# A two-layer encoder trunk on TensorE: combinations issued in steps, tiles 5 to 19 with seven products

## The chip, the cores and the metric

The kernel runs on one core of one Trainium2 chip. The metric is the device time of one execution in microseconds (us). Of the engines, TensorE (PE in the profile) multiplies, VectorE (DVE) and ScalarE (ACT) do elementwise work, GpSimd (POOL) a few squares at the start, and SyncE (SP) issues the loads and stores. PEld is the loading of weights into TensorE, which overlaps its products.

## The reference

Two layers, each a feed-forward stage, a mixer and a second feed-forward stage, on 512 positions of 1024 channels in float32. What matters here is the feed-forward stage, which comes four times:

```python
def swiglu(h, w_gate, w_up, w_down):
    return (jax.nn.silu(h @ w_gate) * (h @ w_up)) @ w_down

for l in range(DEPTH):                      # DEPTH = 2
    f1 = swiglu(rmsnorm(x, ffn1_pre_g[l]), ffn1_w_gate[l], ffn1_w_up[l], ffn1_w_down[l])
    x = x + 0.5 * rmsnorm(f1, ffn1_post_g[l])
    ...                                     # x = x + rmsnorm(mixer_block(rmsnorm(x, ...)), mix_post_g[l])
    f2 = swiglu(rmsnorm(x, ffn2_pre_g[l]), ffn2_w_gate[l], ffn2_w_up[l], ffn2_w_down[l])
    x = x + 0.5 * rmsnorm(f2, ffn2_post_g[l])
```

The hidden width is 2816, so 22 tiles of 128 hidden channels.

## The kernel before, in words

Every float32 operand is cut into a high and a low part (`fp32r`); a product is three matmuls, high by high, high by low and low by high. Weights arrive from memory as raw units of 128 x 1024 (512 KB, one SP DMA each, two pair buffers `raw`). `Weights.prep` cuts them into the tiles `w`, up to AHEAD = 4 steps before they are taken: ACT writes the high part (L163), DVE the low part (L164).

A feed-forward stage (`ffn`) walks over three groups of 7, 7 and 8 hidden tiles. After each group the down projection runs over 8 output tiles (`pd`, and `po` in the last group). There are three ways to make a hidden tile:

- The first three tiles of a stage run in two halves of 256 positions (`hidden` with `halfgemm`, L330 and L331): first all three for the first half, then all three for the second, so that the stage can begin when the first half of its input is there.
- A full tile runs `gemm` twice, for gate and up: 8 blocks x 3 matmuls x 2 = 48 matmuls of 512 columns.
- A tile in the list SEVEN runs `seven`: gate and up and the two position halves form a 2 by 2 block problem that takes seven block products in place of eight, 7 x 4 x 3 = 84 matmuls of 256 columns. It needs sums of weight blocks, made on DVE when the raw unit is cut (L191 to L193, L197, then L201 on ACT and L202 on DVE), and four combinations of input blocks (`comb`), which `combine` makes once a stage. PSUM parts are read between products by ACT (`keep`, L465), and the tile ends on DVE (L478 to L483) and with the cut of `h` (L339 ACT, L340 DVE).

In the kernel before, `combine` is called by the first tile of SEVEN, tile 3, right after the half tiles. It scales the inputs (L427 to L429), forms sums in two buffers of `fa` (L430, L431, L433) and cuts the four results (L436 on ACT, L437 on DVE, 128 x 1024 each).

The order on each engine is set by a list scheduler, which goes through the instructions in the order in which the Python code issues them and lets a ready one pass one that it believes is not ready. Each engine then works its list in order.

At the start, SP loads the first half of x in four pieces, between them the first three weight units, then the second half of x. TensorE runs 12 matmuls of ones (L261) until the first operands are cut. At the end, each output tile of the last stage is added to `fa` in two DVE adds (L561, L562), squared on ACT (L565) and summed into `acc` (L572); a matmul with ones (L353) sums over the partitions, and a chain on ACT and DVE scales the result and stores it (L357 to L382).

Of the kernel before, what the change touches and what calls it, by code (L numbers as in the profile page):

```python
# [9 lines left out]
F32 = mybir.dt.float32  # L10
# [5 lines left out]
L = 2  # L16
# [9 lines left out]
SEVEN = (3, 4, 6, 7, 8, 10, 11, 13, 14, 15, 17, 18, 19)  # L26
AHEAD = 4
LEAD = 3
WARM = 12
# [96 lines left out]
class Weights:  # L126
# [19 lines left out]
    def load(self, pieces=1):  # L146
        i, n = self.loaded, self.units[self.loaded][1]
        if i % 2 == 0:
# [65 lines left out]
def trunk(ctx: ExitStack, tc: tile.TileContext, xt: bass.AP, cst: bass.AP, rows: bass.AP, ws: bass.AP, wp: bass.AP, out: bass.AP):  # L214
# [111 lines left out]
    def halfgemm(ps, w, a, n, ts, ks=None):  # L326
# [23 lines left out]
    def rstd(acc, r, load, steps, eps=None):  # L350
# [64 lines left out]
    def ffn(l, f, xn, rn, acc, fa, end, first):  # L415
# [5 lines left out]
        def combine():  # L421

            q = [v[:, :, :].rearrange("p a (b t) -> p (a b) t", b=2).rearrange("p (u k) t -> p u k t", u=2) for v in fa]
            b12, b22, d, t3 = q[0][:, 0], q[0][:, 1], q[1][:, 0], q[1][:, 1]
            gx = {1: C_F1PRE, 2: C_F2PRE}[f]
            for k in range(4):
# [7 lines left out]
            for v, sign in ((b22, -1.0), (d, 1.0), (t3, 1.0), (b12, -1.0)):  # L434
# [51 lines left out]
        def hidden(m, h, wg, wu, ts, n, first=None):  # L486
# [19 lines left out]
        for gi, g in enumerate(GROUPS):  # L506
# [345 lines left out]
```

## Time and profile before

| | us |
|---|---|
| median of 3 runs (lowest to highest) | 2496.9 (2495.53 to 2497.68) |
| the profiled execution, its own time | 2496.67 |
| its span, first to last instruction | 2494.9 |
| TensorE busy in the span | 2460.0 (99%) |
| VectorE busy | 1658.5 (66%) |
| ScalarE busy | 1223.8 (49%) |

The time of the profiled execution is 1.8 us over its span. TensorE's share of 99% says that it is the engine to follow; matmuls overlap in the pipeline and their ends are modelled, so the share does not show short waits or a lower clock. These are read from single stretches.

### The profile page before, as it was taken

What the parts mean: (1) busy time and instruction counts of PE and PEld (TensorE: products, weight loads), DVE (VectorE), ACT (ScalarE), POOL (GpSimd) and SP (SyncE); (2) the same over time, 40 slices, a digit from 0 to 9 for tenths busy, and PEclk for the clock granted to TensorE, in tenths of its full rate; (3) what the DMA queues carried; (4) which work ended last, traced back from release to release, by engine and by line L of the source; (5) the groups of instructions that cost most, each with busy time, mean ns of one, the idle gap of its engine ahead of it and who ended that gap; (6) DMA issues with size and microseconds to landing.
All of it is one profiled execution on the core that took longest, in us unless ns stands there. A gap on an engine that the chain in (4) does not pass through costs nothing.

```text
span 2494.9 us, 33879 instructions
## 1 busy us (share of the span) xinstructions
PE 2460.0 (99%) x13720; PEld 2155.5 (86%) x13720; DVE 1658.5 (66%) x2480; ACT 1223.8 (49%) x2038; POOL 4.8 (0%) x8
## 2 busy tenths in 40 slices
PE   8999999999999999999999999999999999999998
PEld 7898989888888888989888989898888888889896
DVE  8676774843874586657785667749357846856575
ACT  6443554334773564435564434533357626644343
POOL 0000000000000000000000000000000000000000
PEclk9999999999999999999999999999999999999999
DMA  3323323222223313233212323322213232123231
GB/s 138 110 100 112 119 101 102 81 88 102 90 80 118 118 35 110 100 111 117 88 66 98 110 89 117 130 82 88 101 69 119 89 114 102 49 97 111 87 118 48
DMA packets 69565, 243.52 MB, mean 98 GB/s; under 512 B 7712, under 2 KB 7840, under 8 KB 69408
## 3 DMA queue, kind: packets, MB, share of 16 engines
q1 hardware_dynamic: 69264, 241.20, 27.7%
q8 instruction: 107, 1.75, 0.3%
q14 instruction: 50, 0.41, 0.1%
q10 hardware_dynamic: 144, 0.15, 0.0%
HBM read 239.23 MB, written 2.10 MB: 97 GB/s over the span
## 4 chain that ended last, share of the span: by engine, by line
PE 91%; DVE 5%; ACT 1%; DMA 1%; issue 1%; SPq 0%; DVEq 0%; ACTq 0%
PE po L330 7%; PE pu L309 6%; PE pu L310 6%; PE pu L311 6%; PE pg L310 4%; PE pg L311 4%; PE pg L309 4%; PE pd L309 4%; PE pd L310 4%; PE pd L311 4%; PE po L331 4%; PE pmg L311 3%; PE pmg L309 3%; PE pmg L310 3%; PE py L311 2%; PE py L309 2%
## 5 line engine op out<-in xcount | busy, mean ns | idle before, releaser
L164 DVE TENSOR_TENSOR w<-raw,w 128x1024 fp32r<-128x1024 f32 (+2 forms) x405 | 479.6, 1198 | 155.4 <-ACT w L163 153.3
L163 ACT ACTIVATE w<-raw 128x1024 fp32r<-128x1024 f32 (+2 forms) x405 | 409.0, 1032 | 167.3 <-DMA raw<-wp 58.1
L309 PE MATMUL pg<-xn,w 128*128 128x256 f32 (+1 forms) x608 | 193.1, 318 | 0.0
L310 PE MATMUL pg<-xn,w 128*128 128x256 f32 (+1 forms) x608 | 192.6, 317 | 0.0
L311 PE MATMUL pg<-xn,w 128*128 128x256 f32 (+1 forms) x608 | 192.4, 316 | 0.0
L330 PE MATMUL po<-h,w 128*128 128x512 f32 x512 | 180.2, 396 | 0.0
L309 PE MATMUL pd<-h,w 128*128 128x512 f32 x448 | 174.4, 389 | 0.0
L310 PE MATMUL pd<-h,w 128*128 128x512 f32 x448 | 174.4, 389 | 0.0
L311 PE MATMUL pd<-h,w 128*128 128x512 f32 x448 | 174.3, 389 | 0.0
L309 PE MATMUL pmg<-xn,w 128*128 128x512 f32 x384 | 149.4, 389 | 0.0
L310 PE MATMUL pmg<-xn,w 128*128 128x512 f32 x384 | 149.4, 389 | 0.0
L311 PE MATMUL pmg<-xn,w 128*128 128x512 f32 x384 | 149.4, 389 | 0.0
L331 PE MATMUL po<-h,w 128*128 128x256 f32 x512 | 144.7, 283 | 0.0
L201 ACT ACTIVATE w<-raw 128x512 fp32r<-128x512 f32 x208 | 120.8, 622 | 48.4 <-DVE raw L193 23.6
L202 DVE TENSOR_TENSOR w<-raw,w 128x1024 fp32r<-128x1024 f32 x104 | 125.0, 1222 | 23.6 <-ACT w L201 23.3
L309 PE MATMUL pu<-comb,w 128*128 128x256 f32 x416 | 123.0, 296 | 14.3 <-ACT comb L436 13.5
L311 PE MATMUL pu<-xn,w 128*128 128x256 f32 (+1 forms) x400 | 133.6, 334 | 0.0
L310 PE MATMUL pu<-xn,w 128*128 128x256 f32 (+1 forms) x400 | 133.5, 334 | 0.0
L309 PE MATMUL pu<-xn,w 128*128 128x256 f32 (+1 forms) x400 | 133.4, 334 | 0.0
L310 PE MATMUL pu<-comb,w 128*128 128x256 f32 x416 | 120.7, 290 | 2.7 <-DVE comb L437 2.7
L311 PEld LDWEIGHTS pg<-xn,w 128*128 128x128 f32 x608 | 115.9, 191 | 8.1 <-DVE w L164 0.5
L309 PEld LDWEIGHTS pg<-xn,w 128*128 128x128 f32 x608 | 115.9, 191 | 7.1
(260 smaller groups left out, 6396.0 us busy)
## 6 DMA issues: line engine op xcount, KB each, us to landing
raw<-wp SPq DMA_DIRECT2D x391, 512.0 KB, 4.3
raw<-wp SPq DMA_DIRECT2D x64, 448.0 KB, 4.1
x<-xt SPq DMA_DIRECT2D x8, 256.0 KB, 6.6
out<-x SPq DMA_DIRECT2D x8, 256.0 KB, 2.1
rw<-rows SPq DMA_DIRECT2D x6, 256.0 KB, 3.6
raw<-wp SPq DMA_DIRECT2D x2, 256.0 KB, 4.2
rw<-ws SPq DMA_DIRECT2D x2, 256.0 KB, 4.0
c<-cst ACTq DMA_DIRECT2D x1, 148.0 KB, 4.0
```

The lines of the kernel that those rows point to most:

```text
L163: self.nc.scalar.activation(out=hi, in_=raw, func=AF.Copy)
L164: self.nc.vector.tensor_tensor(out=lo, in0=raw, in1=hi.bitcast(F32), op=ALU.subtract)
L201: self.nc.scalar.activation(out=v[:, 0, b], in_=r[:, n], func=AF.Copy)
L202: self.nc.vector.tensor_tensor(out=v[:, 1], in0=r[:, 0::3] if key[0] == "s1" else r[:, 1:3], in1=v[:, 0].bitcast(F32), op=ALU.subtract)
L309: nc.tensor.matmul(out=ps, lhsT=w_hi, rhs=a_hi, start=first, stop=False, skip_group_check=on)
L310: nc.tensor.matmul(out=ps, lhsT=w_hi, rhs=a_lo, start=False, stop=False, skip_group_check=on)
L311: behind(nc.tensor.matmul(out=ps, lhsT=w_lo, rhs=a_hi, start=False, stop=last, skip_group_check=on))
L330: nc.tensor.matmul(out=ps.rearrange("p (a t) -> p a t", a=2), lhsT=w[:, 0, o:o + 128], rhs=a(k, slice(0, 2), ts), start=k == 0, stop=False)
L331: behind(nc.tensor.matmul(out=ps[:, :HS], lhsT=w[:, 1, o:o + 128], rhs=a(k, 0, ts), start=False, stop=k == n - 1))
```

## The change

Four edits.

1. `combine` becomes a generator, begun before the second half of the half tiles. Its parts are issued after the half tiles 1 and 2 and after each full tile of the first group, in place of all at once in tile 3. Two of the four cuts come after tile 3, two after tile 4. The buffers in `fa` are laid out otherwise; the operations and their sizes are the same.
2. SEVEN is 5 to 19 (15 tiles a stage) in place of 13 tiles from 3 to 19. Tiles 3 and 4 become full tiles, tiles 5, 9, 12 and 16 become seven-product tiles.
3. At the start the first weight unit is loaded in two halves, before and after the second piece of x; units 1 to 3 come after the whole first half of x. 16 matmuls of ones run first, and three more after every second block of the first gate product. The four scalings of constants (L274) wait until the second half of the input is cut.
4. In the last output tile of the second half of the last stage, `gemm` puts all 24 matmuls into one PSUM half, so that one DVE add is enough, and its square goes straight into a second matmul with ones in place of the add to `acc`.

```diff
-SEVEN = (3, 4, 6, 7, 8, 10, 11, 13, 14, 15, 17, 18, 19)
+SEVEN = (5, 6, 7, 8, 9, 10, 11, 12, 13, 14, 15, 16, 17, 18, 19)
-WARM = 12
+WARM = 16
...
             nc.sync.dma_start(out=x_[k // 4][:, h, k % 4:k % 4 + 2], in_=xt[:, h, k:k + 2])
-            if h == 0 and k in (0, 4, 6):
-                wt.load(2 if k == 0 else 1)
+            if h == 0 and k < 4:
+                wt.load(1, 2, k // 2)
+        for i in range(3 if h == 0 else 0):
+            wt.load()
...
+    def busy(n):
+
+        for _ in range(n):
+            nc.tensor.matmul(out=warm[:, :P], lhsT=ones, rhs=ones, start=True, stop=True)
...
+            if k % 2 and k < n - 1:
+                busy(fill)
...
-        mm = nc.tensor.matmul(out=ps, lhsT=ones, rhs=acc, start=True, stop=True)
+        mm = nc.tensor.matmul(out=ps, lhsT=ones, rhs=acc, start=True, stop=more is None)
+        if more is not None:
+            mm = nc.tensor.matmul(out=ps, lhsT=ones, rhs=more, start=False, stop=True)
...
+            yield
             nc.vector.tensor_tensor(out=t3, in0=b22, in1=b12, op=ALU.subtract)
             nc.vector.tensor_tensor(out=b22, in0=b22, in1=d, op=ALU.add)
+            yield
+            parts(b22, -1.0)
+            parts(d, 1.0)
+            yield
+            parts(t3, 1.0)
...
+            parts(b12, -1.0)
+            yield
 
         def seven(m, h):
 
-            if not comb:
-                combine()
...
-                    halfgemm(a, w, xn, KD, ts)
+                    halfgemm(a, w, xn, KD, ts, fill=3 if first and a is pg else 0)
...
+            steps = combine()
             for m in range(skew):
                 hidden(m, h, *ws_[m], HALVES[1], HS)
+                if m > 0:
+                    next(steps)
             for m in range(skew, g):
                 if m0 + m in SEVEN:
                     seven(m, h)
                     continue
                 hidden(m, h, wt.take(("gate", f, l, m0 + m)), wt.take(("up", f, l, m0 + m)), FULL, S)
+                if gi == 0:
+                    next(steps)
...
-                    halfgemm(ps, ws_[d], h, g, ts)
+                    if s and d == 7 and tail:
+                        gemm(ps[:, :HS], ws_[d], h, g, ts)
+                    else:
+                        halfgemm(ps, ws_[d], h, g, ts)
...
-                    nc.vector.tensor_tensor(out=dst, in0=dst, in1=ps[:, HS:], op=ALU.add)
+                    if not (s and d == 7 and tail):
+                        nc.vector.tensor_tensor(out=dst, in0=dst, in1=ps[:, HS:], op=ALU.add)
...
+                elif s and d == 7 and tail:
+                    more = sq
```

How the order moves is seen best in the second feed-forward stage of the first layer. On DVE before, from the end of the half tiles into tile 3 (`comb` are the cut combinations, `a22l` and `raw` the weight unit of tile 4, `fa` the combinations under way, `sg` and `h` the end of the half tiles):

```order
764 L340 TENSOR_TENSOR h<-sg,h 128x256
765 L429 SCALAR_TENSOR_TENSOR fa<-x,c,fa 128x256
766 L430 TENSOR_TENSOR fa<-fa 128x1024
767 L164 TENSOR_TENSOR a22l<-raw,a22h 128x512
768 L431 TENSOR_TENSOR fa<-fa 128x1024
769 L191 TENSOR_TENSOR raw<-raw 128x512
770 L433 SCALAR_TENSOR_TENSOR fa<-x,c,fa 128x256 x4
771 L437 SCALAR_TENSOR_TENSOR comb<-fa,comb 128x1024 x4
772 L192 TENSOR_TENSOR raw<-raw 128x512
```

On DVE now, at the end of tile 3 (its last sum is 790, its `h` 793; `w` and `raw` belong to tile 5):

```order
790 L525 TENSOR_TENSOR sg<-sg,pu 128x512
791 L204 TENSOR_TENSOR w<-raw,w 128x1024
792 L444 SCALAR_TENSOR_TENSOR comb<-fa,comb 128x1024
793 L351 TENSOR_TENSOR h<-sg,h 128x512
794 L444 SCALAR_TENSOR_TENSOR comb<-fa,comb 128x1024
795 L199 TENSOR_TENSOR raw<-raw 128x512
```

Two of the four cuts stand here now. On DVE now, at the end of tile 4 (its last sum is 803, its `h` 806; `w` and `raw` belong to tile 6):

```order
803 L525 TENSOR_TENSOR sg<-sg,pu 128x512
804 L195 TENSOR_TENSOR raw<-raw 128x512
805 L199 TENSOR_TENSOR raw<-raw 128x512
806 L351 TENSOR_TENSOR h<-sg,h 128x512
807 L444 SCALAR_TENSOR_TENSOR comb<-fa,comb 128x1024 x2
808 L204 TENSOR_TENSOR w<-raw,w 128x1024 x2
```

The four cuts stood in one piece between the half tiles and the first tile of SEVEN; the last two now stand behind the last sum of tile 4, ahead of tile 6's weights. On ACT at the same place now (`pt` and `vp` are the reads of PSUM between the products of tile 5):

```order
592 L522 ACTIVATE sg<-sg 128x512
593 L350 ACTIVATE h<-sg 128x512
594 L443 ACTIVATE comb<-fa 128x1024 x2
595 L203 ACTIVATE w<-raw 128x512 x4
596 L165 ACTIVATE w<-raw 128x896
597 L487 ACTIVATE pt<-pu 128x256
598 L487 ACTIVATE vp<-pg 128x256
599 L487 ACTIVATE pt<-pu 128x256
```

Two cuts of combinations and five cuts of weights stand ahead of tile 5's first read of PSUM, behind the end of tile 4. On SP the start before, and then now:

```order
1 L253 DMA x<-xt 128x512
2 L154 DMA raw<-wp 128x512 x2
3 L253 DMA x<-xt 128x512 x2
4 L154 DMA raw<-wp 128x1024
5 L253 DMA x<-xt 128x512
6 L154 DMA raw<-wp 128x1024
7 L253 DMA x<-xt 128x512 x4
```

```order
1 L255 DMA x<-xt 128x512
2 L154 DMA raw<-wp 128x512
3 L255 DMA x<-xt 128x512
4 L154 DMA raw<-wp 128x512
5 L255 DMA x<-xt 128x512 x2
6 L154 DMA raw<-wp 128x1024 x3
7 L255 DMA x<-xt 128x512 x4
```

The four pieces of the first half of x are now issued ahead of all whole weight units, and a third whole unit ahead of the second half of x.

## Rows read from the trace of the kernel before

**Rows 1.** The page's busy times of the whole span.
```profile
PE 2460.0 (99%) x13720; PEld 2155.5 (86%) x13720; DVE 1658.5 (66%) x2480; ACT 1223.8 (49%) x2038; POOL 4.8 (0%) x8
```

**Rows 2.** Windows, second feed-forward stage: tile 8; tile 9; tiles 17 to 19.
```profile
core 0: us, PE busy (x) PEld busy (x) DVE busy (x) ACT busy (x) POOL busy (x), PEclk, DMA share, GB/s
...
1016.36:1026.43 10.07, 10.07 (x86) 10.07 (x85) 9.55 (x15) 7.61 (x13) 0.00 (x0) 1.00 0.29 104
1026.43:1037.34 10.91, 10.91 (x50) 9.02 (x49) 8.03 (x12) 2.42 (x4) 0.00 (x0) 1.00 0.28 98
...
1148.23:1179.10 30.87, 30.87 (x254) 30.44 (x253) 22.89 (x31) 18.25 (x33) 0.00 (x0) 1.00 0.35 119
```

**Rows 3.** Windows: tiles 3, 4 and 5 in each of the four stages.
```profile
45.50:84.10 38.60, 35.00 (x218) 31.92 (x217) 32.41 (x52) 22.15 (x43) 0.00 (x0) 0.91 0.16 51
918.20:958.10 39.90, 34.61 (x218) 31.71 (x217) 34.69 (x56) 24.11 (x47) 0.00 (x0) 0.91 0.16 56
1280.90:1320.20 39.30, 34.41 (x218) 31.41 (x217) 34.70 (x56) 24.12 (x47) 0.00 (x0) 0.91 0.17 57
2153.90:2193.70 39.80, 34.53 (x219) 31.64 (x218) 34.81 (x56) 24.22 (x47) 0.00 (x0) 0.91 0.16 56
```

**Rows 4.** Waits of the whole span: total us, times, longest.
```profile
PE pu L309 <- ACT comb L436: 13.5, 4, 3.9
```

**Rows 5.** Windows: the low clock in tile 3, second stage.
```profile
928.54:935.36 6.82, 5.84 (x25) 5.55 (x26) 6.75 (x8) 3.25 (x6) 0.00 (x0) 0.50 0.00 0
```

**Rows 6.** Timeline (start, us, what), tile 3 of the second stage, DVE and ACT.
```profile
923.77 1.23 DVE L430 TENSOR_TENSOR fa<-fa 128x1024 f32<-128x1024 f32 x1
...
928.83 4.62 DVE L437 SCALAR_TENSOR_TENSOR comb<-fa,comb 128x1024 fp32r<-128x1024 f32 x4
...
926.82 3.90 ACT L436 ACTIVATE comb<-fa 128x1024 fp32r<-128x1024 f32 x4 [2.31 <-DVE fa L431]
```

**Rows 7.** Groups by line: count, busy us, mean ns of one.
```profile
L202 DVE TENSOR_TENSOR w<-raw,w 128x1024 fp32r<-128x1024 f32 x104 | 125.0, 1222 | 23.6 <-ACT w L201 23.3
...
L480 DVE TENSOR_TENSOR sg<-sg,rn 128x512 f32<-128x512 f32 x52 | 35.8, 688 | 1.0
...
L483 DVE SCALAR_TENSOR_TENSOR sg<-sg,vp 128x256 f32<-128x256 f32 x52 | 21.8, 418 | 0.0
```

**Rows 8.** Timeline of DVE, tiles 17 to 19 of the second stage.
```profile
1158.78 0.69 DVE L480 TENSOR_TENSOR sg<-sg,rn 128x512 f32<-128x512 f32 x1
1159.38 0.69 DVE L164 TENSOR_TENSOR a22l<-raw,a22h 128x512 fp32r<-128x512 f32 x1
...
1166.18 1.22 DVE L164 TENSOR_TENSOR w<-raw,w 128x1024 fp32r<-128x1024 f32 x1
1167.32 0.42 DVE L478 TENSOR_TENSOR vp<-vp 128x256 f32<-128x256 f32 x1
...
1169.89 0.42 DVE L483 SCALAR_TENSOR_TENSOR sg<-sg,pu 128x256 f32<-128x256 f32 x1 [0.70 <-ACT sg L481]
```

**Rows 9.** Timeline of the start: PE, ACT.
```profile
1.05 5.49 PE L261 MATMUL warm<-ones 128*128 128x128 f32 x24 [1.05 <-DVE ones L258]
6.46 0.70 PE L330 MATMUL pg<-xn,w 128*128 128x512 f32 x1
...
14.03 0.40 PE L330 MATMUL pu<-xn,w 128*128 128x512 f32 x1
...
10.09 0.91 ACT L388 ACTIVATE xn<-x,c 128x256 fp32r<-128x256 f32 x2 [0.94 <-DMA x<-xt]
```

**Rows 10.** Windows: the start's stretch at the low clock.
```profile
10.36:13.77 3.41, 3.24 (x9) 2.44 (x10) 3.41 (x6) 3.41 (x7) 0.81 (x1) 0.50 1.06 404
```

**Rows 11.** Chain of waits at the end: start, us, what.
```profile
2482.00 0.43 DVE fa L561
...
2483.36 0.44 DVE acc L572
2483.84 0.71 PE st L353 x2
```

More of the change, by code (lines that the diff above doesn't have):

```diff
@@ L151, in load @@
         of = self.wp[self.off:self.off + P * n].rearrange("(p n) -> p n", p=P)
-        for j in range(pieces):
-            part = slice(n * j // pieces, n * (j + 1) // pieces)
-            self.nc.sync.dma_start(out=raw[:, part], in_=of[:, part])
+        part = slice(n * a // pieces, n * (a + count) // pieces)
+        self.nc.sync.dma_start(out=raw[:, part], in_=of[:, part])
+        if a + count < pieces:
+            return
         self.raw[i] = self.pair
@@ L259, in trunk @@
     warm = st_p.tile([P, S], F32, tag="st", name="warm")
-    for i in range(WARM):
-        nc.tensor.matmul(out=warm[:, :P], lhsT=ones, rhs=ones, start=i == 0, stop=i == WARM - 1)
+    def busy(n):
+        for _ in range(n):
+            nc.tensor.matmul(out=warm[:, :P], lhsT=ones, rhs=ones, start=True, stop=True)
+    busy(WARM)
     def col(l, j):
@@ L267, in after, with halved @@
         tc.add_manual_dep(a.ins, b.ins.name, mybir.DependencyInfo(mybir.DependencyClass.NoSync, mybir.DependencyReason.DATA), reason="table set")
-    def halved():
+    def halved(last):
         for l in range(L):
@@ L273, in halved @@
                 v = c[:, l * NC + j:l * NC + j + 8]
-                nc.vector.tensor_scalar(out=v, in0=v, scalar1=0.5, scalar2=None, op0=ALU.mult)
+                after(nc.vector.tensor_scalar(out=v, in0=v, scalar1=0.5, scalar2=None, op0=ALU.mult), last)
     def derived(last):
@@ L324, in gemm, with halfgemm @@
             mm3(ps, w[:, 0, o:o + 128], w[:, 1, o:o + 128], a(k, 0, ts), a(k, 1, ts), k == 0, k == n - 1)
-    def halfgemm(ps, w, a, n, ts, ks=None):
+    def halfgemm(ps, w, a, n, ts, ks=None, fill=0):
         for k in ks or range(n):
@@ L348, in roots, with rstd @@
         return load
-    def rstd(acc, r, load, steps, eps=None):
+    def rstd(acc, r, load, steps, eps=None, more=None):
         ps = st_p.tile([P, S], F32, tag="st", name="st")[:, :HS]
-        mm = nc.tensor.matmul(out=ps, lhsT=ones, rhs=acc, start=True, stop=True)
+        mm = nc.tensor.matmul(out=ps, lhsT=ones, rhs=acc, start=True, stop=more is None)
+        if more is not None:
+            mm = nc.tensor.matmul(out=ps, lhsT=ones, rhs=more, start=False, stop=True)
         later.append([steps, mm])
@@ L372, in bc, with post @@
         return v[:, None, :].to_broadcast([P, 2, HS])
-    def post(fa, acc, ts, load, store):
+    def post(fa, acc, ts, load, store, more=None):
         r = t2("r1")[:, :HS]
-        rstd(acc[:, ts], r, load, 0 if store else 4 if ts is HALVES[0] else 9)
+        rstd(acc[:, ts], r, load, 0 if store else 4 if ts is HALVES[0] else 9, more=more)
         for n, (i, js) in enumerate(PAIRS):
@@ L388, in cut @@
             nc.scalar.activation(out=xn(k, 0, ts), in_=yk, func=AF.Copy, scale=gk)
-            nc.vector.scalar_tensor_tensor(out=xn(k, 1, ts), in0=yk, scalar=gk, in1=xn(k, 0, ts).bitcast(F32), op0=ALU.mult, op1=ALU.subtract)
+            low = nc.vector.scalar_tensor_tensor(out=xn(k, 1, ts), in0=yk, scalar=gk, in1=xn(k, 0, ts).bitcast(F32), op0=ALU.mult, op1=ALU.subtract)
+        return low
     def scale(ts, scratch, r, steps, load=False, first=False, eps=None):
@@ L421, in combine, with parts @@
         def combine():
-            q = [v[:, :, :].rearrange("p a (b t) -> p (a b) t", b=2).rearrange("p (u k) t -> p u k t", u=2) for v in fa]
+            q = [v.rearrange("p (u b) (k t) -> p u (b k) t", u=2, k=2) for v in fa]
             b12, b22, d, t3 = q[0][:, 0], q[0][:, 1], q[1][:, 0], q[1][:, 1]
             gx = {1: C_F1PRE, 2: C_F2PRE}[f]
+            def parts(v, sign):
+                t = slot_p.tile([P, 2, 4, HS], F32R, tag="slot", name="comb")
+                nc.scalar.activation(out=t[:, 0], in_=v, func=AF.Copy, scale=sign)
+                nc.vector.scalar_tensor_tensor(out=t[:, 1], in0=v, scalar=sign, in1=t[:, 0].bitcast(F32), op0=ALU.mult, op1=ALU.subtract)
+                comb.append(t)
             for k in range(4):
@@ L537, in out_halves @@
     def out_halves(l, gp, g, h, key, fa, acc, add, end):
-        ws_ = []
+        ws_, more, tail = [], None, key[:3] == ("down", 2, L - 1)
         for s, ts in enumerate(HALVES):
@@ L570, in out_halves @@
                     nc.vector.scalar_tensor_tensor(out=acc[:, ts], in0=acc[:, ts], scalar=E8, in1=sq, op0=ALU.add, op1=ALU.add)
+                elif s and d == 7 and tail:
+                    more = sq
                 elif d > 0 or add:
                     nc.vector.tensor_tensor(out=acc[:, ts], in0=acc[:, ts], in1=sq, op=ALU.add)
-            end(s, acc, load if s == 0 else None)
+            end(s, acc, load if s == 0 else None, more)
     def mixer(l, xn, fa, end):
@@ L789, in cuts @@
         for n, (i, js) in enumerate(PAIRS):
-            cut(n, l, g, xn, ts, xs(i, js, ts))
+            last = cut(n, l, g, xn, ts, xs(i, js, ts))
+        return last
     for n, (i, js) in enumerate(PAIRS):
@@ L800, in rest, with chain @@
     def rest():
-        cuts(0, gains[0], xn, HALVES[1])
+        last = cuts(0, gains[0], xn, HALVES[1])
         root = scale(HALVES[1], scratch, rn[:, HALVES[1]], 0, eps=acc[:, HALVES[1]])
-        halved()
+        halved(last)
         return root
     decay = []
-    def chain(ts, acc, load, nxt, fa, box):
-        post(fa, acc, ts, load, nxt is None)
+    def chain(ts, acc, load, more, nxt, fa, box):
+        post(fa, acc, ts, load, nxt is None, more)
         if nxt is not None:
@@ L825, in trunk, with end @@
         box = {}
-        def end(half, acc, load, nxt=nxt, fa=fa, box=box):
+        def end(half, acc, load, more, nxt=nxt, fa=fa, box=box):
             ts = HALVES[half]
-            chain(ts, acc, load, nxt, fa, box)
+            chain(ts, acc, load, more, nxt, fa, box)
         if s == 1:
```

9 lines of the change are left out of this document (2 added, 7 removed).

## The prediction

> **What bounds the kernel now.** I read the busy times first. TensorE is busy 99% of the span, VectorE 66%, ScalarE 49% [rows 1]: time is won only by giving TensorE fewer columns, fewer waits or a higher clock. Then I cut a feed-forward stage into windows at the first matmuls of its tiles, to see what a tile costs when nothing is late. A full tile takes 10.91 us with PEld busy 9.02 us of it; a seven-product tile takes 10.07 us with PEld busy all the time [rows 2] (two of the counted matmuls in each window belong to the neighbours). So 84 matmuls of 256 columns run at 0.120 us each, 48 of 512 at 0.227, and a tile that changes kind saves 0.84 us.
>
> The same windows around the first seven-product tiles look otherwise. Tiles 3, 4 and 5 are two of seven products and a full one, 2 x 10.07 + 10.91 = 31.05 us. They take 38.60, 39.90, 39.30 and 39.80 in the four stages [rows 3], 157.6 together, 33.4 us over 4 x 31.05. The waits name the cause: TensorE waits for ACT's cut of the combinations (L436) once in each stage, 13.5 us in all, up to 3.9 at a time [rows 4]. The timeline shows why they are late: tile 3 begins at 918.20 [rows 3], the first combined sum (L430) starts on DVE at 923.77, ACT idles 2.31 us for the second, then four cuts follow on ACT until 930.7 and on DVE until 933.4 [rows 6], while TensorE needs them one by one. The wait is not all: in the middle of it the granted clock is 0.50, that is 1.2 GHz in place of 2.4, for 6.82 us [rows 5], which doubles the matmuls in it. The clock fell after TensorE had stood still for those 3.9 us. Waits and low clock together are the 33.4 us.
>
> **The change part by part.** The sum is made against the profiled execution's own 2496.67 us (0.2 under the median of 2496.9).
>
> *Combinations.* In time order the cuts now stand two at the end of tile 3 and two behind the last sum of tile 4, and the first seven-product tile is tile 5. Two full tiles (21.8 us) lie between the half tiles and their first use. Is DVE through by then? Consecutive DVE instructions start 0.60 us apart at 512 columns and 1.14 at 1024 [rows 8]. Before, DVE was 5.6 us behind at L430 (923.77 against 918.20); it had cut a seven-product unit during the half tiles (five instructions of 0.60, four of 1.14 with its neighbours: 7.6 us), and now cuts four plain units (4.6), so about 2.6 us behind. From there to tile 4's last sum the order has 8 instructions of 1024 columns, 12 of 512 and 9 of 256 (about 0.4): 9.1 + 7.2 + 3.6 = 19.9. 2.6 + 19.9 = 22.5, against 21.8 at which tile 4's products end: DVE is just in time. The first two combinations are cut at the end of tile 3 and cannot be late. What can be late is ACT: behind tile 4's `h` it has two cuts of combinations (0.97 each, from 3.90 for four [rows 6]), four half cuts and one plain cut of weights (about 0.5 and 0.9 by their widths), 5 us in all, and only then tile 5's first read of PSUM, which TensorE needs before the third product into that bank, 56 matmuls x 0.120 = 6.7 us after tile 4. With DVE at 22.5 and 1.2 us for sum and `h` that read is done about 7.1 us after tile 4, 0.4 late. Bounds: 0 a stage if DVE keeps up, 3.9 if it is still 5.6 behind. I take 0.6, the nearer end, 2.4 us for four stages. -33.4 + 2.4 = -31.0.
>
> *Seven-product tiles.* 15 in place of 13 in each of four stages: 8 x 0.84 = -6.7 us. What hides their preparation is DVE's slack, and there is little. A tile needs 3 DVE instructions of 1024 columns, 8 of 512 and 3 of 256. By their starts that is 3 x 1.14 + 8 x 0.60 + 3 x 0.42 = 9.5 us of the 10.07, as tile 8 shows (9.55 busy [rows 2]). The weights of a tile are cut during the second last tile before it, so a DVE that is late by a microsecond is not seen. A run of three, tiles 17 to 19, took 30.87 us, 0.66 over 3 x 10.07 [rows 2]: ACT's reads of PSUM stood for moments behind a cut. Now there are runs of seven (7 to 13) and six (14 to 19) with a down projection ahead of each. If a run loses 0.66 once, the two lose 0.66 more a stage than now, +2.6; if each further tile loses its 0.22, thirteen tiles lose 2.9 and the addition is 2.2 a stage, +8.8; nothing at best. I take 2.6.
>
> Here a rule speaks against the change. The rows show that DVE starts an instruction 0.60 us after one that lasts 0.69 [rows 8], so they overlap. The Trainium skill ("VectorE: DVE Perf Modes", "The DRAIN you can't avoid") says that the next DVE operation does not start before the pipe is empty. By that rule a tile would cost the sum of the whole durations, the second rival below; the trace does not bear it out. The skill also gives an isolated matmul gap of N/2.4 + 2.5 ns ("TensorE: Matmul & The Clock Gate", "Back-to-back issue gap"), 0.109 us at 256 columns and 0.216 at 512: a tile would save 48 x 0.216 - 84 x 0.109 = 1.2 us and the eight 9.6 in place of 6.7 (an estimate by that page); the measured 0.120 and 0.227 decide.
>
> *Start.* TensorE's first product starts at 6.46 and the first gate tile ends at 14.03 [rows 9], though its 8 x (0.23 + 0.12) us of work are 2.8. It waited for x, whose last piece reached ACT at 10.09 [rows 9], and ran at clock 0.50 from 10.36 to 13.77 [rows 10]. Now a weight unit less stands ahead of that piece, 512 KB at the 404 GB/s of [rows 10], 1.3 us, and 9 matmuls of ones fill the waits. 16 matmuls ahead are 32 records in place of 24: at the 5.41/24 = 0.225 us of [rows 9] they end at 8.3, if the last ones run at full clock (0.12 or less) at 7.4. 7.4 + 2.8 + 18 fill records x 0.12 = 12.4, 1.6 us earlier than 14.03, provided the clock stays up, as the fill lets TensorE stand still nowhere. With everything at 0.225: 8.3 + 2.8 + 4.1 = 15.2, 1.1 later. At best the gate ends with its last operands, some 3 us earlier. I take -1.6. The constants' scalings move to where DVE has finished the second half's cuts; the next reader is microseconds away, cost 0.
>
> *End.* The last output tile costs 24 x 0.12 = 2.9 in place of 2.8 (+0.1), saves one DVE add (0.43) and the add to `acc` (0.44) in the chain [rows 11]; the matmul over `acc` runs while the last square is made, and the one over the square replaces it (0.71). -0.8; between -0.4, if the second pair of records stands behind the first, and -0.9.
>
> Sum: -31.0 - 6.7 + 2.6 - 1.6 - 0.8 = -37.5, 2496.67 - 37.5 = 2459.2. I say 2459.
>
> **The rivals.** *The combinations stay late.* The scheduler put two cuts behind tile 4's last sum, and ACT's first PSUM read behind them. If DVE is as far behind as before, TensorE waits 3.9 us in each tile 5 and the clock falls again, 3.4 us more by half of 6.82. That is 7.3 in place of 0.6, four times: 2459 + 27 = 2486. For it: DVE ends the half tiles behind. Against: 3 us less to cut there, and 21.8 us of full tiles. Half a failure, one of the two parts, gives 2472.
>
> *The runs become DVE's.* Whole durations are 3 x 1.222 + 8 x 0.688 + 3 x 0.418 = 10.42 us a tile [rows 7]. If they do not overlap, 60 tiles lose 0.35 each, 2459 + 21 = 2480. (It is what the rule of the Trainium skill above would make of the change.) The case ends on the slow side if DVE also waits in each tile as it did at the end of the run of three, 0.70 for ACT's silu [rows 8], and as much again for the cut of `h`: 11.8 us a tile, 1.7 over TensorE's, for the 52 tiles of the long runs 90 us, 2549. It decides from 37.5/52 = 0.72 us a tile on, a DVE cycle of 10.8 us. Against it: tile 8's 9.55, and these waits fell where DVE had nothing else ready.
>
> *Little comes of it* because the low clock has another cause and stays: then only the waits go, 13.5 + 6.7, 2476.
>
> **How the numbers follow.** Forecast, 2451 to 2472: 0.80. Its low end has no wait in tile 5, no loss in the runs and the best start, 2459.2 - 2.4 - 2.6 - 1.4 = 2452.8, and a microsecond or two of the small losses that the stages have elsewhere; its high end the worst of the runs (+6.2), of the start (+2.7) and 1 us more in each tile 5 (+4). Combinations late in full or half, or a clock that stays low, 2472 to 2492: 0.13. DVE's cycle: 0.04, three quarters of it slow. Better than 2451: 0.03. Leaving out 0.20 in all, I give 2450 to 2472 as the range. A measurement of this kernel can tell about 0.2%, 5 us, from no change. Faster is everything below 2492: 0.95; within 0.2%: 0.02 (late combinations and a lossy run together); slower 0.03.
>
> **What would show it.** In the profile after: no wait of TensorE for a cut of `comb` above a microsecond; granted clock 1.00 in all windows of tiles 3 to 5; 10.91 for tiles 3 and 4; the runs 7 to 13 and 14 to 19 within 1 us of 70.5 and 60.4; DVE near 9.5 us in each of their tiles; the first `pu` product at 12 to 13 us; the last square to the ACT read of the sum under 1.2 us. I am wrong if TensorE waits in the runs for `w`, or if the clock still falls in tile 5.

## The result and the profile after

The changed kernel takes 2453.65 us (median of 4 runs, 2453.39 to 2453.74) beside 2496.64 us for the kernel before on the same chip: ratio 0.9828, 95% interval 0.9811 to 0.9845. It is 43.0 us faster; forecast were 37.5 us and 2459. The profiled execution took 2453.64 with a span of 2451.8, so 43.1 less than the span before.

The page's busy times of the whole span, as in [rows 1]:

```profile
PE 2437.9 (99%) x14044; PEld 2155.7 (88%) x14044; DVE 1693.0 (69%) x2550; ACT 1243.3 (51%) x2102; POOL 5.0 (0%) x8
```

TensorE has 324 matmul records more and is 22 us less busy: fewer columns, and none of them at the low clock. The windows of the changed kernel, with the columns of [rows 2]: tiles 3 to 5 of the four stages, then of the second stage tile 5, the run 7 to 13, the run 14 to 19, and tile 8.

```profile
45.55:77.81 32.26, 32.26 (x183) 28.19 (x181) 29.05 (x40) 17.46 (x29) 0.00 (x0) 1.00 0.16 50
908.48:940.73 32.25, 32.25 (x183) 28.19 (x181) 30.05 (x43) 19.27 (x34) 0.00 (x0) 1.00 0.14 45
1260.24:1292.47 32.23, 32.23 (x182) 28.19 (x181) 29.96 (x42) 18.97 (x33) 0.00 (x0) 1.00 0.15 47
2122.71:2154.97 32.26, 32.26 (x183) 28.20 (x182) 30.06 (x43) 19.29 (x34) 0.00 (x0) 1.00 0.14 48
...
930.26:940.73 10.47, 10.47 (x86) 10.17 (x84) 8.89 (x11) 7.21 (x12) 0.00 (x0) 1.00 0.32 104
988.90:1059.45 70.55, 70.55 (x589) 70.55 (x588) 58.92 (x85) 39.67 (x77) 0.00 (x0) 1.00 0.33 113
1097.56:1158.13 60.57, 60.57 (x505) 60.51 (x504) 50.07 (x72) 34.40 (x65) 0.00 (x0) 1.00 0.33 113
998.97:1009.05 10.08, 10.08 (x86) 10.08 (x85) 9.58 (x15) 6.23 (x12) 0.00 (x0) 1.00 0.20 62
```

Compare the first four with [rows 3]: 129.0 us in place of 157.6, the granted clock 1.00 in place of 0.91. The runs cost 7 x 10.08 and 6 x 10.08 us plus 0.1: PEld is busy all the time. Waits of TensorE and of its weight loads in the changed kernel (total us, times, longest), the largest of each apart from the warm-up:

```profile
PE pg L340 <- DVE w L166: 0.8, 1, 0.8
```

```profile
PEld pu L318 <- ACT pt L487: 1.1, 6, 0.2
```

The wait for the cut of a combination [rows 4] is gone. The second row is a kind of wait that the forecast did not read: a weight load of TensorE held back by ACT's read of PSUM (`pt`). In the kernel before, that view says:

```profile
PEld pu L309 <- ACT pt L465: 3.8, 14, 0.8
```

Of these 14, five lie in tiles 3 to 5, eight (0.2 us each) in tiles 10 and 17, and one in tile 15. Of the 6 in the changed kernel four lie in tile 5, one a stage, and none in tiles 10 and 17.

The 43.1 us by the forecast's terms; "measured" is the difference of the two profiled executions:

| term | forecast | measured | from |
|---|---|---|---|
| combinations | -31.0 | -32.0 | 157.6 - 4 x 31.05 = 33.4 before; 129.0 - 4 x 31.89 = 1.4 after |
| 8 more seven-product tiles | -6.7 | -6.7 | 8 x (10.91 - 10.07) |
| runs of seven-product tiles | +2.6 | -3.9 | what tiles 6 to 19 take over 10.08 and 10.91 each: 4.7 before, 0.7 after, rounded |
| start | -1.6 | +0.1 | tile 3 of the first stage begins at 45.55, before at 45.50 |
| end | -0.8 | -0.8 | chain below -0.9, products of the last tile +0.1 |

(31.89 = 2 x 10.91 + 10.07, since tiles 3 and 4 are full now.) The rest, 0.2, lies in the half tiles. The surplus over the forecast, 5.6 us, is one term of the wrong sign, the runs (6.5), and 1.0 more from the combinations, less one gain that was not there, the start (1.7).

What tile 5 still loses is 0.4 us a stage, at two places. ACT at the end of tile 4 and in tile 5 of the third stage, then PEld there (start, us, what):

```profile
1283.54 1.99 ACT L443 ACTIVATE comb<-fa 128x1024 fp32r<-128x1024 f32 x2
1285.43 2.18 ACT L203 ACTIVATE w<-raw 128x512 fp32r<-128x512 f32 x4
1287.52 0.94 ACT L165 ACTIVATE w<-raw 128x896 fp32r<-128x896 f32 x1
1288.36 0.36 ACT L487 ACTIVATE pt<-pu 128x256 f32<-128x256 f32 x1
...
1290.51 0.38 ACT L487 ACTIVATE pt<-pu 128x256 f32<-128x256 f32 x1 [1.52 <-PE pu L320]
```

```profile
1290.94 0.19 PEld L318 LDWEIGHTS pu<-comb,w 128*128 128x128 f32 x1 [0.20 <-ACT pt L487]
```

The first read of `pt`, at 1288.36, stands behind the queue of cuts that the forecast wrote down. It costs 0.15 us: TensorE's next product into that bank starts 0.05 late, at 1288.77. The second read, at 1290.51, stands behind no other work: ACT had been idle for 1.52 us and starts it when its product ends. But TensorE's list has only four matmuls between that product and the next one into the same bank, so it waits all the same, and this place costs 0.26 us. The forecast did not have it. At both places the held matmul and its weight load start together (1290.94 at the second), and the matmul behind them comes 0.22 us later in place of 0.12. These 0.10 us are in the two sums.

The end, chain of waits of the changed kernel, as in [rows 11]:

```profile
2439.89 0.43 DVE fa L593
...
2440.34 0.42 ACT sq L596
...
2440.81 0.71 PE st L366 x2
...
2441.54 0.39 ACT rt L370
```

From the last product to the first scaling it is 3.91 us (2439.86 to 2443.77, L392), before 4.82 (2481.98 to 2486.80).

The start: VectorE and GpSimd of the changed kernel.

```profile
6.60 1.53 DVE L166 TENSOR_TENSOR w<-raw,w 128x512 fp32r<-128x512 f32 x1
8.05 2.44 DVE L402 SCALAR_TENSOR_TENSOR xn<-x,c,xn 128x256 fp32r<-128x256 f32 x2
```

```profile
6.33 3.88 POOL L411 TENSOR_TENSOR scr<-x 128x512 f32<-128x512 f32 x3 [0.33 <-DMA x<-xt]
```

Three cuts take 1.53, 1.26 and 1.26 us (the last two overlap a little, 2.44 together) where the same forms take 0.69 and 0.47 elsewhere, just while GpSimd squares x. TensorE's first `pu` product comes at 13.75, before at 14.03 [rows 9].

### The profile page after: what moved, and what is told of

Read it like the earlier page. It is cut to its first block, busy times and chain, and to the rows that moved or that the text cites. A ratio compares the mean times of both kernels' runs of the same rounds, so it can differ in the third digit from the quotient of the medians.

```text
span 2451.8 us, 34684 instructions
## 1 busy us (share of the span) xinstructions
PE 2437.9 (99%) x14044; PEld 2155.7 (88%) x14044; DVE 1693.0 (69%) x2550; ACT 1243.3 (51%) x2102; POOL 5.0 (0%) x8
## 4 chain that ended last, share of the span: by engine, by line
PE 98%; DVE 1%; ACT 0%; DMA 0%; issue 0%; SPq 0%; DVEq 0%
PE po L339 7%; PE pu L318 6%; PE pu L320 6%; PE pu L319 6%; PE pg L318 5%; PE pg L319 5%; PE pg L320 5%; PE pd L318 4%; PE pd L320 4%; PE pd L319 4%; PE po L340 4%; PE pmg L319 4%; PE pmg L320 4%; PE pmg L318 4%; PE py L319 2%; PE py L318 2%
## 5 line engine op out<-in xcount | busy, mean ns | idle before, releaser
L166 DVE TENSOR_TENSOR w<-raw,w 128x1024 fp32r<-128x1024 f32 (+2 forms) x397 | 470.8, 1199 | 135.1 <-ACT w L165 133.0
L165 ACT ACTIVATE w<-raw 128x1024 fp32r<-128x1024 f32 (+2 forms) x397 | 401.4, 1032 | 132.0 <-DMA raw<-wp 45.3
L318 PE MATMUL pg<-xn,w 128*128 128x256 f32 (+1 forms) x608 | 185.8, 306 | 0.0
L319 PE MATMUL pg<-xn,w 128*128 128x256 f32 (+1 forms) x608 | 185.7, 305 | 0.0
L320 PE MATMUL pg<-xn,w 128*128 128x256 f32 (+1 forms) x608 | 185.7, 305 | 0.0
L203 ACT ACTIVATE w<-raw 128x512 fp32r<-128x512 f32 x240 | 141.5, 623 | 65.6 <-DVE raw L195 24.8
L204 DVE TENSOR_TENSOR w<-raw,w 128x1024 fp32r<-128x1024 f32 x120 | 142.4, 1220 | 17.6 <-ACT w L203 17.6
L318 PE MATMUL pu<-comb,w 128*128 128x256 f32 x480 | 137.2, 286 | 0.0
L320 PE MATMUL pu<-comb,w 128*128 128x256 f32 x480 | 135.8, 283 | 0.0
L319 PE MATMUL pu<-comb,w 128*128 128x256 f32 x480 | 135.7, 283 | 0.0
L318 PEld LDWEIGHTS pg<-xn,w 128*128 128x128 f32 x608 | 116.2, 191 | 5.1
L320 PEld LDWEIGHTS pg<-xn,w 128*128 128x128 f32 x608 | 116.2, 191 | 5.0
L319 PEld LDWEIGHTS pg<-xn,w 128*128 128x128 f32 x608 | 116.2, 191 | 4.7
L320 PE MATMUL pu<-xn,w 128*128 128x256 f32 (+1 forms) x368 | 117.7, 320 | 0.0
```

What stands on the lines that cost most here:

```text
L165: self.nc.scalar.activation(out=hi, in_=raw, func=AF.Copy)
L166: self.nc.vector.tensor_tensor(out=lo, in0=raw, in1=hi.bitcast(F32), op=ALU.subtract)
L203: self.nc.scalar.activation(out=v[:, 0, b], in_=r[:, n], func=AF.Copy)
L204: self.nc.vector.tensor_tensor(out=v[:, 1], in0=r[:, 0::3] if key[0] == "s1" else r[:, 1:3], in1=v[:, 0].bitcast(F32), op=ALU.subtract)
L318: nc.tensor.matmul(out=ps, lhsT=w_hi, rhs=a_hi, start=first, stop=False, skip_group_check=on)
L319: nc.tensor.matmul(out=ps, lhsT=w_hi, rhs=a_lo, start=False, stop=False, skip_group_check=on)
```

## The experiments

"Before" is the kernel before, run beside each of these on the same chip (2495.4 to 2496.1 us). Small differences are read against the changed kernel's 2453.65. The medians of "before" differ by up to 0.7 us from one group of experiments to the next, so a difference below 1 us counts only where the profile shows its place.

**1. The combinations alone** (old start, old end, 12 seven-product tiles a stage).

```diff
-SEVEN = (5, 6, 7, 8, 9, 10, 11, 12, 13, 14, 15, 16, 17, 18, 19)
+SEVEN = (5, 6, 7, 8, 10, 11, 13, 14, 15, 17, 18, 19)
...
```

> Combinations in steps with the old start and the old end, and twelve seven-product tiles a stage: 5 to 8, 10, 11, 13 to 15, 17 to 19. Tiles 9, 12 and 16 stay full, tiles 3 and 4 become full, tile 5 becomes a seven. Theory A (the gain is the combinations' waits and the low clock behind them; 0.38 us stays in each tile 5, as in the changed kernel): 2496.6 - 33.4 + 1.5, and four times one seven-product tile fewer at 0.84 us, +3.4: 2468. Theory B adds that part of the surplus of the changed kernel over the forecast comes from something else than the combinations, namely that a seven-product tile behind a full tile loses 0.4 to 0.5 us: then the first tiles of the runs 10, 13 and 17 still lose here, and the time is that of A; if the losses were those of the old combinations, tile 10 and tile 17 lose nothing here and the time is 2464.

2469.06 (2468.37 to 2470.49), before 2495.70; ratio 0.9894 (0.9878 to 0.9911). The time that A and B share, and B's tiles 10 and 17 (tile 13 loses nothing). Tiles 3 to 5 lose 1.5 us in all, as in the changed kernel, while tiles 6 to 19 lose 4.8, as in the kernel before (4.7). Windows of the second stage: tile 10, tiles 17 to 19; and PEld's wait for `pt`:

```profile
1025.14:1035.98 10.84, 10.74 (x85) 10.22 (x84) 6.95 (x7) 7.48 (x13) 0.00 (x0) 1.00 0.44 153
1136.20:1167.07 30.87, 30.87 (x253) 30.43 (x252) 22.88 (x31) 18.16 (x33) 0.00 (x0) 1.00 0.34 117
```

```profile
PEld pu L319 <- ACT pt L488: 2.6, 13, 0.2
```

The second window is the 30.87 of [rows 2] again, to the hundredth. Eight of the 13 waits lie in tiles 10 and 17 again. So the losses belong to the list with full tiles in between, not to the old combinations. The 26.6 us are 1.9 fewer than A's sum of 28.5; in the profile the start has them: tile 3 of the first stage begins at 47.33, in the kernel before at 45.50.

**2. Distance without steps**: all of `combine` in front of tile 5.

```diff
-                if m > 0:
-                    next(steps)
...
                 if m0 + m in SEVEN:
+                    for _ in steps if gi == 0 else ():
+                        pass
                     seven(m, h)
```

> The changed kernel with all of the combinations issued at once in front of tile 5. Theory (they must be issued ahead of their first use; the two full tiles in front of tile 5 do not help by themselves): TensorE waits in tile 5 as it did in tile 3, some 2 us less because VectorE is nearer to its place there; waits and a stretch at granted clock 0.50 come back in every tile 5, 20 to 31 us in all, 2474 to 2485. Rival (it is enough that two full tiles let VectorE catch up): no stretch at low clock, 2454 to 2458.

2478.11 (2476.91 to 2479.11), ratio to before 0.9931 (0.9916 to 0.9946): the theory. Tiles 3 to 5 of the second stage, and the waits:

```profile
914.54:952.45 37.91, 34.91 (x182) 30.58 (x181) 28.08 (x42) 18.30 (x34) 0.00 (x0) 0.91 0.08 25
```

```profile
PE pu L318 <- ACT comb L443: 10.5, 4, 2.6
```

**3. Steps without distance**: SEVEN from 3 to 17, two steps in the half tiles, the rest in front of tile 3.

```diff
+SEVEN = (3, 4, 5, 6, 7, 8, 9, 10, 11, 12, 13, 14, 15, 16, 17)
...
                 if m0 + m in SEVEN:
+                    for _ in steps if gi == 0 else ():
+                        pass
                     seven(m, h)
```

> The changed kernel with fifteen seven-product tiles from 3 to 17: two steps of the combinations are issued in the half tiles, the rest in front of tile 3. Theory (VectorE needs the two full tiles to get through): the four cuts follow the sums in one piece, TensorE waits 1 to 3 us in each tile 3 and the clock falls there: 10 to 25 us over the changed kernel, 2464 to 2479. Rival (issuing in steps is all): 2454 to 2456.

2484.79 (2484.32 to 2485.33), ratio 0.9958 (0.9943 to 0.9973), above the theory's range. Of the 10.9 us under before most is the seven-product tiles and their runs; the steps alone win almost nothing. Tiles 3 to 5, second stage, and the waits:

```profile
914.43:952.99 38.56, 32.89 (x255) 32.00 (x253) 37.73 (x61) 26.39 (x54) 0.00 (x0) 0.91 0.17 59
```

```profile
PE pg L318 <- ACT comb L443: 16.0, 4, 4.3
```

Over their tiles' own cost the windows of tiles 3 to 5 lose, four stages together: 33.4 before, 33.0 with steps alone, 23.0 with distance alone (and 2.9 more in tile 6), 1.4 with both. Alone the steps are worth 0.4 us and the distance 7.5, together 32.0.

**4. Waiting without the low clock**: the kernel before, with matmuls of ones ahead of the wait in tile 3.

```diff
+            if len(comb) == 4 and not filled:
+                ...
+                for _ in range(18):
+                    nc.tensor.matmul(out=ones_on[:, :P], lhsT=ones, rhs=ones, start=True, stop=True)
             product(a, of(w2), 0, n2, False)
```

> The kernel before with 18 matmuls of ones (128 columns, 0.20 us each) in the first seven-product tile of each stage, where TensorE stands still for the combinations. Nothing is made ready earlier. Theory (the low clock comes from the standing still, and half of its 6.82 us is lost): the waits stay, the clock stays at 1.00 in tile 3, 4 x 3.4 = 13.6 us less than before, 2483. Rival (the low clock has another cause): the clock falls as before and the time is 2496 or more.

2491.85 (2490.68 to 2495.57), ratio 0.9985 (0.9976 to 0.9994): between the two. Windows of tile 3 in the first three stages, then in the fourth:

```profile
46.20:60.40 14.20, 14.20 (x122) 14.09 (x121) 13.96 (x25) 9.88 (x21) 0.00 (x0) 1.00 0.00 0
916.00:932.10 16.10, 14.70 (x122) 14.28 (x121) 16.02 (x30) 11.57 (x26) 0.00 (x0) 1.00 0.05 17
1278.30:1294.10 15.80, 14.61 (x123) 14.21 (x122) 15.72 (x29) 11.23 (x24) 0.00 (x0) 1.00 0.02 7
2149.50:2167.20 17.70, 16.30 (x122) 15.76 (x121) 16.66 (x30) 11.66 (x26) 0.00 (x0) 0.90 0.05 17
```

In three stages the clock stayed at 1.00 (0.80 to 0.81 before) and tile 3 took 2.2 to 2.6 us less (before 16.8, 18.4, 18.0). So in three stages the low clock went with the long wait, as the theory says; the 3.4 was mis-sized, since in 1.6 of the 6.82 us at the low clock (928.54 to 930.10) the trace has one matmul, and TensorE otherwise waited for two more cuts. By this, as an estimate, 4 x 2.4 = 9.6 of the 33.4 us were the clock and 24 the waits. In the fourth stage the clock fell all the same, though TensorE stood for 0.56 and 0.84 us there, just as in the second, where it did not fall; why is open. 3.9 of the 7.8 us won in the four tiles show in the time; some of the rest went to a slower start (tile 3 begins at 46.2) and 1.2 us more in tile 10 of the second stage.

**5. The old start.**

```diff
-WARM = 16
+WARM = 12
...
-                halfgemm(a, w, xn, KD, ts, fill=3 if first and a is pg else 0)
+                halfgemm(a, w, xn, KD, ts, fill=0)
```

(and the old order of loads and of the scalings.)

> The changed kernel with the start of before: the old order of loads, 12 matmuls of ones, none in the first gate product, the scalings of constants not held back. The forecast's term would make this 1.6 us slower, 2455.2. Theory from the trace of the changed kernel (its first product waits for VectorE, whose cuts take 1.25 us in place of 0.47 while GpSimd squares beside it, in both orders of loads): no difference, 2453.2 to 2454.0.

2454.47 (2453.94 to 2455.07): 0.8 slower, between theory and forecast. Windows of 10 to 16 us, with the old start and in the changed kernel:

```profile
10.00:16.00 6.00, 5.48 (x16) 4.05 (x15) 6.00 (x9) 6.00 (x13) 1.51 (x2) 0.50 0.72 267
```

```profile
10.00:16.00 6.00, 5.38 (x33) 4.51 (x34) 6.00 (x10) 5.52 (x10) 0.20 (x1) 1.00 0.78 280
```

The low clock stands here for all 6 us, some 6.8 in all, as in experiments 1 and 4; in the profiled execution of before it was 3.41 [rows 10], the shortest of the four profiles with the old start. In this profile tile 3 of the first stage begins at 47.09, in the changed kernel at 45.55, in before at 45.50. So the new start wins 1.5 us against an execution with the long stretch, nothing against that of before, and 0.8 by the medians.

**6. The fill matmuls left out of the new start.**

```diff
-                    halfgemm(a, w, xn, KD, ts, fill=3 if first and a is pg else 0)
+                    halfgemm(a, w, xn, KD, ts, fill=0)
```

> The changed kernel without the 18 matmuls of ones in its first gate product; its order of loads and the 16 matmuls ahead stay. Theory (the fills keep the clock up: each profiled execution with the old start had a stretch at granted clock 0.50 there, of 3.4 to 7 us): TensorE stands still for the cuts, the clock falls to 0.50 between 9 and 17 us, and the time is that of the old start, 2454.2 to 2455. Rival (the order of loads keeps the waits short enough): the clock stays at 1.00, 2453.6.

2453.78 (2453.35 to 2454.14): the rival. The same window has TensorE less busy and the clock still at 1.00:

```profile
10.00:16.00 6.00, 4.40 (x22) 3.00 (x21) 6.00 (x10) 5.43 (x10) 0.41 (x1) 1.00 0.77 279
```

The fills win nothing that shows. (They are 9 matmuls, 18 records of the profile; the expectation calls the records matmuls.) Whether the order of loads or the 16 matmuls ahead keep the clock up was not separated.

**7. Squares on ScalarE at the start.**

```diff
-    scale(HALVES[0], scratch, rn[:, HALVES[0]], 0, first=True, eps=acc[:, HALVES[0]])
+    scale(HALVES[0], scratch, rn[:, HALVES[0]], 0, eps=acc[:, HALVES[0]])
```

> The changed kernel with the four squares of the first half of x on ScalarE in place of GpSimd. Theory (GpSimd beside it holds VectorE up: three instructions of 1.53, 1.26 and 1.26 us where 0.68, 0.47 and 0.47 are usual, 2.4 us): the first gate product ends up to 2.4 us earlier, the first up product starts at 11.5 to 12.5 in place of 13.75, and the time is 1.2 to 2.2 us less, 2451.4 to 2452.5. Rival (the loads set the start: weight unit 1 reaches ScalarE at 9.97): VectorE is faster and TensorE waits for the weights, 2453.6.

2452.07 (2451.91 to 2452.26), 1.6 less; tile 3 of the first stage begins at 43.98 in place of 45.55. The cuts of VectorE at the same place, and the first `pu` product:

```profile
6.52 0.69 DVE L166 TENSOR_TENSOR w<-raw,w 128x512 fp32r<-128x512 f32 x1
7.13 0.88 DVE L402 SCALAR_TENSOR_TENSOR xn<-x,c,xn 128x256 fp32r<-128x256 f32 x2
```

```profile
11.97 0.40 PE L339 MATMUL pu<-xn,w 128*128 128x512 f32 x1
```

GpSimd was what held the start. The Trainium skill ("SBUF — State Buffer", "SBUF: two separate sides") says that GpSimd shares a port pair with a VectorE instruction that has two inputs in SBUF, and that whichever comes first holds it to its end. The trace agrees: in the kernel before, the last square takes 1.04 us, as alone, and the cut that starts beside it takes 1.26 in place of 0.47 and ends 0.28 after the square:

```profile
10.13 1.04 POOL L397 TENSOR_TENSOR scr<-x 128x512 f32<-128x512 f32 x1
10.19 1.26 DVE L389 SCALAR_TENSOR_TENSOR xn<-x,c,xn 128x256 fp32r<-128x256 f32 x1
```

**8. The old end.**

```diff
-        ws_, more, tail = [], None, key[:3] == ("down", 2, L - 1)
+        ws_, more, tail = [], None, False
```

> The changed kernel with the end of before: two adds in the last output tile and its square added to the sum before one matmul with ones. Forecast and trace agree on 0.8 (0.91 us less in the chain from the last product to the scaling, 0.1 more in the products): 2454.4. Rival: the end is set elsewhere, 2453.6.

2454.50 (2454.30 to 2455.17): 0.85 slower, as forecast. In its profile, the slowest of the four runs, the way from the last product to the first scaling takes 5.17 us in place of 3.91.

**9. Tile 10 full.**

```diff
-SEVEN = (5, 6, 7, 8, 9, 10, 11, ...
+SEVEN = (5, 6, 7, 8, 9, 11, ...
```

> The changed kernel with tile 10 as a full tile, so the run 7 to 13 is cut in two. Theory A (a run costs its tiles alone): 4 x 0.84 = +3.4, 2457.0. Theory B (a seven-product tile behind a full tile loses 0.4 to 0.5 us, because the full tile hands ScalarE and VectorE their work at its end): tile 11 shows an excess of 0.4 to 0.5 us in each stage and the time is 2458.6 to 2459. The forecast's own theory (each run loses 0.66 through its length): the shorter runs give back up to 2.6, 2454.4.

2458.35 (2457.40 to 2459.00), 4.7 slower, of which 3.4 is the tile: near B's time, at another place. Windows of the third stage, tile 9 and tile 11, then PEld's wait in tile 9 and ACT ahead of it:

```profile
1362.73:1373.52 10.79, 10.44 (x86) 10.18 (x85) 9.28 (x15) 5.20 (x10) 0.00 (x0) 1.00 0.36 140
1384.43:1394.50 10.07, 10.07 (x85) 10.06 (x84) 5.29 (x8) 3.69 (x7) 0.00 (x0) 1.00 0.29 91
```

```profile
1369.11 0.19 PEld L318 LDWEIGHTS pu<-comb,w 128*128 128x128 f32 x1 [0.55 <-ACT pt L487]
```

```profile
1368.16 0.63 ACT L203 ACTIVATE w<-raw 128x512 fp32r<-128x512 f32 x1 [0.64 <-DVE raw L193]
1368.69 0.36 ACT L487 ACTIVATE pt<-pu 128x256 f32<-128x256 f32 x1
```

Tile 11, behind the full tile, loses nothing; tile 9, ahead of it, lost 0.0, 0.1, 0.7 and 0.1 in the four stages. "Behind a full tile" falls as a rule, and one gap costs 0.2 us a stage on average, most of it in one stage. In that tile 9 ACT's read of `pt` (1368.69) stands behind a cut of weights (1368.16) that had itself waited for VectorE. A full tile in the run shifts the cuts (three preparation steps a seven-product tile, two a full one); that this shift puts the cut there is argued, not shown.

**10. and 11. Longer runs**, with the squares on ScalarE: tile 20, then 20 and 21.

```diff
+SEVEN = (5, 6, 7, 8, 9, 10, 11, 12, 13, 14, 15, 16, 17, 18, 19, 20)
...
+SEVEN = (5, 6, 7, 8, 9, 10, 11, 12, 13, 14, 15, 16, 17, 18, 19, 20, 21)
...
```

> The changed kernel with the squares on ScalarE at the start (as in the run that moved them) and tile 20 as a sixteenth seven-product tile. Theory (a run of seven-product tiles costs its tiles alone, and VectorE, 4.9 us busy in tile 20 as a full tile, has room): 2452.1 - 4 x 0.84 = 2448.7, tiles 14 to 20 at 10.08 us each. The forecast's theory (each further tile of a run loses 0.22): 2449.6. Rival (the weights of the output projection, which are cut during tiles 20 and 21, come late): the output stage starts with a wait, 2450 to 2452.

> As the run before it, and tile 21, the last ahead of the output projection, with seven products too. Theory: 3.4 us less again, 2445.3; the end of a seven-product tile on VectorE and ScalarE (some 5 us) is covered by the 3 x 7 blocks of the output projection that do not need tile 21 (3 x 7 x 0.35 = 7.4 us). Rival (VectorE has tile 21's end, the weights of the output projection and its first sums at once): TensorE waits 1 to 3 us at the head of each output projection, 2449 to 2457.

2448.70 (2448.54 to 2448.79) and 2445.74 (2445.61 to 2446.99): 3.4 and 3.0 less, the theory both times. Tiles 14 to 20 of the second stage, in the first of the two:

```profile
1095.77:1166.32 70.55, 70.55 (x589) 70.55 (x588) 59.42 (x86) 39.00 (x75) 0.00 (x0) 1.00 0.35 120
```

Seven tiles at 10.08: a longer run costs its tiles alone.

**12. One full tile ahead**: as 11, with tile 4 too.

```diff
+SEVEN = (4, 5, 6, 7, 8, 9, 10, 11, 12, 13, 14, 15, 16, 17, 18, 19, 20, 21)
...
                 if m0 + m in SEVEN:
+                    for _ in steps if gi == 0 else ():
+                        pass
                     seven(m, h)
...
```

> As the run with tiles 20 and 21, and tile 4 as well, so one full tile stands between the half tiles and the first use of the combinations; all steps are issued ahead of tile 4. Theory (22.5 us of VectorE's work need two full tiles): the third and fourth combination are late in tile 4, TensorE waits 1 to 3 us a stage and, where it stands longest, the clock falls: 2446 to 2456 in place of 2445.7. Rival (one full tile is enough): 2445.7 - 3.4 = 2442.4.

2445.24 (2444.27 to 2446.19), 0.5 under 11, with overlapping runs: ratio to before 0.9797 (0.9783 to 0.9810), the lowest measured. TensorE has no listed wait for a combination; VectorE starts to cut the fourth at 923.36, 7.6 us into tile 4 of the second stage. The theory's waits of 1 to 3 us fall. Of the rival's 3.4 us the profiles show 1.4 and the medians 0.5. Two stages lose 0.67 us in tiles 4 to 6, where run 11 loses 0.4 in tile 5, and in three stages the first down projection loses some 0.26, since its products wait for the cut of `h`:

```profile
PEld pd L319 <- DVE h L351: 1.3, 3, 0.4
```

## Why the prediction was right, and where it was not

*What bounds the kernel* was read rightly: TensorE's waits for the combinations and the clock behind them were the largest thing to win. Experiment 1 takes that part alone, with one seven-product tile given up: -26.6 measured, -28.5 worked out, the difference being the start of that execution. Experiments 2 and 3 show that the change needs both its parts. Of the signs that the prediction named, all came but one, the first `pu` product at 12 to 13 us.

*Combinations*, -31.0 forecast, -32.0 measured. The clock stayed up in all four tiles 5. Of the working, VectorE's 22.5 us were too many. In the changed kernel it is ready for tile 4's last sum before TensorE's product is, in all four stages; in the third, where tile 3 begins at 1260.24:

```profile
1282.28 0.69 DVE L525 TENSOR_TENSOR sg<-sg,pu 128x512 f32<-128x512 f32 x1 [0.23 <-PE pu L320]
```

That is 22.04 us after the begin, 21.13 of them busy. So ACT's first read of `pt` ended 6.7 us after tile 4 in place of the 7.1 worked out, almost in time. That tile 5 loses 0.4 us, near the 0.6 that the forecast took, is partly luck: only 0.15 come from the queue that it reckoned with, 0.26 from the order of TensorE's products at the second read.

*Seven-product tiles*: 0.84 us each, again in experiments 10 (3.4 for four) and 11 (3.0). By the isolated gap of the Trainium skill ("TensorE: Matmul & The Clock Gate", "Back-to-back issue gap") it would have been 1.2 each, an estimate; the runs show that the measured 0.120 and 0.227 us are the ones to use for this stream of weight loads and products.

*The runs* are the step that failed. "A run of three, tiles 17 to 19, took 30.87 us, 0.66 over" was right as a reading, but it was one run of the four that each stage of the kernel before has, and the price was hung on it as a price of a run's length. The others stood in the same trace. Tiles 10 and 11, then 14 and 15, of the second stage before:

```profile
1037.34:1058.06 20.72, 20.72 (x169) 20.28 (x168) 16.06 (x22) 11.30 (x21) 0.00 (x0) 1.00 0.26 96
1117.15:1137.31 20.16, 20.16 (x170) 20.15 (x169) 14.53 (x21) 10.87 (x20) 0.00 (x0) 1.00 0.31 106
```

The shorter run loses 0.56 us, the pair out of a longer one nothing (2 x 10.08 = 20.16), so length is not the price. And even at 0.66 a run, two runs in place of four would have been a gain of 1.3 a stage and not a loss. The loss goes with the full tiles in between: 4.8 us with three of them (experiment 1), 0.7 without. Most of it lies in tiles 10 and 17, the first behind a full tile, 0.4 to 0.8 us each, mostly at the same two places as in tile 5 now: a first read of `pt` behind five cuts of weights, a second with four matmuls to cover it. Why tile 13, which also follows a full tile, loses nothing is open, and experiment 9 shows that a single gap can cost as little as 0.1. By sign the term was +2.6 for -3.9, 6.5 us, more than the whole surplus of 5.6.

*The slow rival*, VectorE setting the pace, was tested by the runs themselves. VectorE's whole durations are 10.42 us a tile [rows 7], the tiles take 10.08, VectorE is busy 9.58 of it: consecutive instructions overlap. The prediction quotes the rule of the pipe without its exception. The same page of the Trainium skill ("VectorE: DVE Perf Modes") says in "Two Vector instructions with no wait between them" which instructions are held until the earlier ones have finished; the overlap here agrees with instructions that are not held.

*Start*, -1.6 forecast. The first `pu` product came at 13.75 for 12 to 13; against the profiled execution nothing was won, by the medians of experiment 5 0.8. The fills were credited with keeping the clock up, and it stays up without them (experiment 6). The forecast counted only TensorE's records; the cuts that TensorE waits for were slowed by GpSimd's squares, in both orders, and showed in the kernel before too (its cuts of 1.1 to 1.26 us from 7.98 on). Removing that gave 1.6 (experiment 7).

*End*, -0.8: as worked out, and again in experiment 8; from the end of the last square to ACT's read of the sum it is 0.78 us.

## What to carry to other kernels

Work that is needed once a stage has to be issued both early enough and in pieces; before believing that one of the two suffices, undo the other. When a repeated pattern is interrupted, look at what the interruption costs before adding up what the pattern costs: here the even run was free, and three interruptions cost 1.2 us a stage. Read the weight load's waits as well as the matmul's, and where an engine is slow for no reason of its own, look at what GpSimd does at that moment.

## What the runs showed of the hardware that was not expected

A VectorE cut of 256 columns takes 0.47 us alone and 1.10 to 1.26 beside a GpSimd square, one of 512 columns 0.69 and 1.53. GpSimd's squares, 1.04 us alone, take 1.22 to 1.35 in the changed kernel where they and the cuts alternate. Behind a matmul that had to wait for a read of PSUM the next one comes 0.22 us later in place of 0.12, and the weight load of the held one starts together with it. The granted clock fell to 0.50 in experiment 4's fourth stage, though TensorE had stood no longer than 0.84 us at a time; it did not fall in the second stage with the same waits, nor in experiment 6 with waits of 0.94, 0.45, 0.56 and 0.39 us one after another.
